# A hybrid decoder layer on one core: single-row states decayed by Scalar and added in one piece, two attention components' scores in one bank, a mask added as a product, and the end of memory attention in another order

## The chip, the cores and the metric

The kernel runs on one core of a Trainium2 chip. The metric is the device time of one execution in microseconds; before the change three runs gave 938.86, 939.27 and 941.57 us, a median of 939.27.

The engines have short names in what follows: PE is TensorE, the matrix engine, with PEld for its weight loads; DVE is VectorE, ACT is ScalarE, POOL is GpSimd, and SP is SyncE, whose queue issues nearly all DMAs. Each engine works through its own list of instructions in order, and waits where the next one's inputs or buffers are not ready.

## The reference, cut to what matters

One layer of a decoder trunk is computed for a prompt (512 tokens) and for 8 samples of 4 new tokens each, with the same weights. The four places that the change touches compute this:

```python
# 1. mLSTM heads (4 x 128): state of each sample and head
C_new = decay[..., None, None] * C + jnp.einsum('bhsd,bhse->bhde', wk, vc)

# 2. differential attention (4 heads, two components c of 64 dims)
s = jnp.einsum('bqhcd,bkhcd->bhcqk', q, k) * (DA_QK_DIM ** -0.5)
s = jnp.where(mask, s, -jnp.inf)
p = jax.nn.softmax(s, axis=-1)
a = p[:, :, 0] - lam * p[:, :, 1]
return jnp.einsum('bhqk,bkhd->bqhd', a, v)

# 3. attention to 256 memory tokens (4 heads x 256), then w_mo
p = jax.nn.softmax(jnp.einsum('bqhd,bkhd->bhqk', q, k) * (MEM_HEAD_DIM ** -0.5), axis=-1)
o = jnp.einsum('bhqk,bkhd->bqhd', p, mv).reshape(B, T, D_MODEL)
return o @ w_mo
```

The prompt's mask is causal (a query sees keys up to its own position). A sample's queries see 256 cached keys and, causally, its 4 new ones. A gated feed-forward part with a depthwise convolution over time follows; its convolution state, weights and bias are small arrays.

## The kernel before

The layer runs in stages on one core, with the matrix engine as the common thread: the mixer's input projection and the mLSTM heads (to 244 us), differential attention (244 to 300), its output projection, memory attention (430 to 475), the w_mo projection (from 476), and the feed-forward part to the end. Products of the projections are made in three terms of two-part numbers: a weight tile in f32 (`wst`, 512 KB by DMA) is cast by ScalarE into a high part and by VectorE, which subtracts that, into a low part, both in a slot `wslot` (four slots, lines 146 and 147). The product lines 411, 412 and 413 use them.

PSUM is split into two pools: five banks tagged "mm" (`mmp`) and three tagged "at" (`at`). A tile of a pool waits until the user of its bank that many tiles ago has been read. Six stage buffers of 4 KB a partition hold `wst` tiles. The order of each engine's list is not the order of the code: a scheduler with a timeline of its own picks it, within the data's dependences, priorities, and `tc.issue_after(x)`, which keeps what is recorded in it behind the instruction x.

The places that the change touches:

- **mLSTM state of the samples** (`mls_update`, lines 1002 to 1011). Eight pieces (two groups of four samples, four heads). Each is one product `mlus` (line 1006) into an "at" bank and four VectorE instructions of 128 columns (line 1008), one for each sample, that multiply its state (held in a `wst` buffer) by its decay and add its part of the product. The state then goes out by DMA and frees its buffer.
- **Differential attention of the prompt** (`da_soft`, lines 1247 to 1265): 16 units, a unit being a block of 128 queries and one head, with 128, 256, 384 or 512 keys. For each of the two components one bank `sda` gets the scores (line 1256) and, by a product of the identity with the mask `cb` in bf16 (line 1257), the mask on the last 128 keys. VectorE takes the row maximum (line 1259), ScalarE the exponentials (line 1260), VectorE joins the components (line 1264); later units of the pipe transpose the result (`tpa`, line 1272, copied to `aT` by line 1274) and multiply by the values (`oda`, line 1284).
- **Differential attention of the samples** (`dk_turn`, `dk_scores`, lines 1220 to 1245): cached keys are transposed (`tpk`, line 1228, copied to `kT` by ScalarE and VectorE in turn, line 1229); the scores `ssc` of two samples each (line 1241) get the mask of the new tokens by a VectorE add of 128x4 (line 1244).
- **Memory attention.** The prompt's part is a pipe of eight units: scores `sca` (line 1454), exponentials `cp` (line 1461), transposes `cpt` (line 1473), values `cpo` (line 1485). Between them stand the samples' scores `ssc` (`mk_scores`, line 1527, from `wst` and `kvt` tiles of the cache), their sum and softmax (`mem_softmax`, with the transposes `spt` and the copies `caz`, line 1576), and their values `pso` (`mv_out`, line 1593): first the values that lie in `wst` buffers, then those in `kvt`. Code lines 1644 to 1659 set how the prompt's pipe and `pso` alternate; `NMID` is 3 and sets how many steps of the pipe come between the softmax and `pso`.
- **Loads around it.** `W.pump()` requests the first four tiles of w_mo. `cr` gets the convolution's state, weights and bias by 24 small DMAs (`conv_in`, lines 1674 to 1676); seven transposes `cvp` (line 1688) read it behind the first matmuls of w_mo. `before` (line 1140) loads five blocks `xb` of the residual for the sum behind w_mo.

Of the kernel before, what the change touches and what calls it, by code (L numbers as in the profile page):

```python
# [7 lines left out]
F32 = mybir.dt.float32  # L8
# [7 lines left out]
P = 128  # L16
# [3 lines left out]
TS = 4  # L20
NS = NB * TS
ROWS = SEQ + NS
H = 4
# [54 lines left out]
def kernel(ctx: ExitStack, tc: tile.TileContext, I, O):  # L78
# [146 lines left out]
    def slotA(w, k0, n0, nrow=256, share=False):  # L225
        def emit():
            st, s = v2(stage(), 512), slot_tile()
            sv = s.rearrange("p l (k n) -> p l k n", k=2)
            r0 = k0 * P
            if nrow == 256:  # L230
                dma(out=st, in_=w[r0:r0 + 256, n0:n0 + 512].rearrange("(k p) n -> p k n", p=P))
                split_w(sv, st, share)
            else:
                dma(out=st[:, 0, :], in_=w[r0:r0 + P, n0:n0 + 512])
                for p0 in (0, 64):
                    dma(out=st[p0:p0 + 64, 1, :], in_=w[r0 + P:r0 + P + 64, n0:n0 + 512])
                split(sv[:, 0], sv[:, 1], st)
            return sv, st
        W.add(emit)
# [113 lines left out]
    class Fill:  # L353
# [8 lines left out]
        def run(self, amount=1e9):  # L362
            while amount > 0 and self.q:
                try:
                    amount -= next(self.q[0])
                except StopIteration:
                    self.q.pop(0)
# [634 lines left out]
    def mls_update(i):  # L1002
        g, h = i // H, i % H
        cs_t = csts[g, h]
        pu = at("mlus")
        mm(pu, lhsT=kS[:, h, :], rhs=vzs[i], start=True, stop=True)
        for b in range(4):
            STT(out=cs_t[:, b, :], in0=cs_t[:, b, :], scalar=dec[:, h, 4 + 4 * g + b:5 + 4 * g + b], in1=pu[:, b * P:(b + 1) * P],
                op0=MUL, op1=ADD)
        dma(out=O["s_ml_C"][0, 4 * g:4 * g + 4, h].rearrange("b d e -> d b e"), in_=cs_t)  # L1010
        F.run(2.5)

    run(pipe(2 * H, mls_values, lambda i: None, lambda i: None, mls_update))
    r, ss = gq[:, 14:15], gq[:, 15:16]
    STT(out=r, in0=den, scalar=-1.0, in1=den, op0=MUL, op1=MAX)
    VTT(out=r, in0=r, in1=gq[:, 2:3], op=MAX)
# [102 lines left out]
    def proj_add(xt, gname, src, gname2, dst, order=None, scale=None):  # L1119
# [20 lines left out]
        def before(b):  # L1140
            for c in [4, 0, 1, 2, 3] if scale else [b]:
                if c not in xb:
                    xb[c] = N("xb")[:rows(c)[1]]
                    dma(out=xb[c], in_=src(c))

        def ev1(b, ps):
            c0, n = rows(b)
# [74 lines left out]
    def dk_turn(b):  # L1222
        kt = kts[b] = wp.tile([P, H, 260], F32, name="kT", tag="W")
        nc.gpsimd.tensor_copy(out=kt[:, :, 256:260], in_=dkT[:, :, SEQ + TS * b:SEQ + TS * (b + 1)])
        for g in range(2):
# [2 lines left out]
                tr(ps[:, h * P:(h + 1) * P], kst[b][g][:, h * P:(h + 1) * P], ident)  # L1228
            (VCP if g else nc.scalar.copy)(out=kt[:, :, g * P:(g + 1) * P], in_=v2(ps, P))

    def dk_scores(b):

        if b % 2 == 0:
            return
        pair = {}
        t = None
        for c in (b, b - 1):
            pair[c] = mmp("ssc")[:, :260]
            for h in range(H):
                with burst(t):  # L1240
                    t = mm(pair[c][NS * h:NS * h + NS], lhsT=qz[:, h, c // 4].rearrange("p c r -> p (c r)"), rhs=kts[c][:, h, :],
                           start=True, stop=True).ins
        for c, ps in pair.items():
            VTT(out=ps[:, 256:260], in0=ps[:, 256:260], in1=con("cm4"), op=ADD)
            sample_exp(sall, c, ps, nm, su)

    def da_soft(i):
        b, h = i // H, i % H
        c0 = b * P
        nk = c0 + P  # L1250
        pt = pts[i] = N("pda").rearrange("p (c k) -> p c k", c=2)
        nm = small(2, "nm")
        su = small(2, "su")
        sv = [mmp("sda")[:, :nk] for _ in range(2)]
        for c in range(2):
            mm(sv[c], lhsT=(dqz if c else dqT)[:, h, c0:c0 + P], rhs=dkT[:, h, 0:nk], start=True, stop=False)
            mm(sv[c][:, c0:nk], lhsT=identb, rhs=cmaskb, start=False, stop=True)
        for c in range(2):
            VRED(out=nm[:, c:c + 1], in_=sv[c], axis=AX.X, op=MAX, negate=True)
            ACT(out=pt[:, c, :nk], in_=sv[c], func=AF.Exp, bias=nm[:, c:c + 1], accum_out=su[:, c:c + 1])  # L1260
        rc = sm.tile([P, 2], F32, name="rc", tag="rc", bufs=6)
        nc.vector.reciprocal(out=rc, in_=su)
        VTS(out=rc[:, 1:2], in0=rc[:, 1:2], scalar1=su[:, 0:1], scalar2=nlam, op0=MUL, op1=MUL)
        STT(out=pt[:, 0, :nk], in0=pt[:, 1, :nk], scalar=rc[:, 1:2], in1=pt[:, 0, :nk], op0=MUL, op1=ADD)
        rcs[i] = rc
# [138 lines left out]
    for t in qx[0] + [both]:  # L1404
        nc.gpsimd.memset(t, 0.0)
    qh, ql = [], []
    selG = cst.tile([P, P], F32, name="selG")
    s32 = T2([P, 32], "selg")
    VRED(out=v2(s32, TS), in_=ident.rearrange("p (n g t) -> p n t g", n=NB, g=4), axis=AX.X, op=ADD)
    VCP(out=selG.rearrange("p (n g t) -> p n g t", n=NB, g=4), in_=v2(s32, TS).unsqueeze(2).broadcast_to([P, NB, 4, TS]))  # L1410
# [98 lines left out]
    def mk_scores(bs):  # L1509

        t = None
        ps = {b: mmp("ssc")[:, :256] for b in bs}
        for e in range(2):
            if e and bs[0] == 0:
                next(prompt)
# [127 lines left out]
    mk_sum(t)  # L1643
    with tc.high_priority():
        mem_softmax()
    for _ in range(NMID):
        next(prompt, None)
    pso = mmp("pso")[:, :256]
    for n0 in (0, 512):
# [1 line left out]
    W.nslots = NSLOT  # L1651
    mv_out(VORD[:6])
    W.pump()
    next(prompt, None)
    next(prompt, None)
    mv_out(VORD[6:])
    run(prompt)
    oS = Z("oS")[:, :256]
    nc.scalar.copy(out=oS, in_=pso)
    ps = at("ost")  # L1660
# [16 lines left out]


    cr = N("cr")
    for g in range(6):  # L1680
        conv_in(cr, 20 * g, 0, 896 * g + (64 if g > 2 else 0), 896)
    conv_in(cr, 0, 896, 2688, 64)
    conv_in(cr, 0, 960, 5440, 64)
    for t0 in (0, 4):
        ps = at("cvp")
        nt = min(4, 7 - t0)
# [372 lines left out]
```

## Time and profile before

| | value |
| --- | --- |
| median of three runs | 939.27 us |
| the profiled execution's own time | 938.97 us |
| span of its profile | 937.2 us |
| mean granted clock of TensorE | 0.994 |
| VectorE, ScalarE, GpSimd busy | 65%, 40%, 24% of the span |
| TensorE waits from 244 to 300 us | 3.1 us in all |
| TensorE waits from 430 to 482 us | 4.2 us in all |
| TensorE waits from 482 us to the end | 0.3 us |

Times in the profile count from the span's start. A wait is the time in which an engine stands still and what released it; "PE mm L411 <- ACT wslot L146" is TensorE at line 411, released by ScalarE's write of wslot in line 146. The granted clock is the share of TensorE's full speed that its throttle let through; a matmul at half the clock takes twice as long and still counts as busy. The time of a row in the timeline includes the pipeline's depth, so that the starts of two matmuls lie closer than one lasts.

### The profile page before, as it was taken

What the parts mean: (1) busy time and instruction counts of PE and PEld (TensorE: products, weight loads), DVE (VectorE), ACT (ScalarE), POOL (GpSimd) and SP (SyncE); (2) the same over time, 40 slices, a digit from 0 to 9 for tenths busy, and PEclk for the clock granted to TensorE, in tenths of its full rate; (3) what the DMA queues carried; (4) which work ended last, traced back from release to release, by engine and by line L of the source; (5) the groups of instructions that cost most, each with busy time, mean ns of one, the idle gap of its engine ahead of it and who ended that gap; (6) DMA issues with size and microseconds to landing.
All of it is one profiled execution on the core that took longest, in us unless ns stands there. A gap on an engine that the chain in (4) does not pass through costs nothing. (4 is left out here: it accounts for less than half of the span.)

```text
span 937.2 us, 17472 instructions
## 1 busy us (share of the span) xinstructions
PE 914.7 (98%) x6780; PEld 798.0 (85%) x6780; DVE 607.5 (65%) x1128; ACT 377.7 (40%) x728; POOL 223.4 (24%) x475
## 2 busy tenths in 40 slices
PE   8999999999999999999999999999999999999995
PEld 5899787879866778998767899889988998999974
DVE  5845144565887438687545778637747785776767
ACT  5745233344586447724434533332212222222232
POOL 6611000024442116581000553001100110110114
PEclk9999999999999999999999999999999999999998
DMA  8950023335780439956766632062054304412023
GB/s 282 320 182 5 1 90 138 91 105 159 246 294 7 137 117 299 321 189 232 283 231 166 202 116 69 26 180 69 22 140 133 89 10 116 133 49 90 24 94 118
DMA packets 120834, 130.59 MB, mean 139 GB/s; under 512 B 8599, under 2 KB 86264, under 8 KB 120752
## 3 DMA queue, kind: packets, MB, share of 16 engines
q1 hardware_dynamic: 114568, 125.96, 42.5%
q10 hardware_dynamic: 6184, 3.53, 1.2%
q8 instruction: 53, 0.87, 0.4%
q14 instruction: 29, 0.24, 0.1%
HBM read 112.54 MB, written 16.93 MB: 138 GB/s over the span
## 5 line engine op out<-in xcount | busy, mean ns | idle before, releaser
L146 ACT CAST wslot<-wst 128x1024 fp32r<-128x1024 f32 x125 | 130.7, 1049 | 265.5 <-issue 72.6
L485 PE MATMUL mm<-fT,wslot 128*128 128x256 f32 x1872 | 235.9, 288 | 0.0
L485 PEld LDWEIGHTS mm<-fT,wslot 128*128 128x128 f32 x1872 | 234.4, 188 | 1.8 <-issue 0.8
L147 DVE TENSOR_TENSOR wslot<-wst,wslot 128x1024 fp32r<-128x1024 f32 x125 | 154.5, 1239 | 85.4 <-ACT wslot L146 84.8
L1865 PE MATMUL mm<-wslot,act 128*128 128x512 f32 (+1 forms) x180 | 69.3, 387 | 0.0
L1868 PE MATMUL mm<-wslot,act 128*128 128x512 f32 (+1 forms) x172 | 67.1, 391 | 0.0
L1869 PE MATMUL mm<-wslot,act 128*128 128x512 f32 (+1 forms) x172 | 66.8, 392 | 0.0
L1767 POOL COPY cvo<-u 128x2 f32<-128x2 f32 x43 | 10.4, 242 | 217.1 <-DVE u L1765 217.1
L411 PE MATMUL mm<-wslot,hT 128*128 128x512 f32 x128 | 51.3, 402 | 0.0
L413 PE MATMUL mm<-wslot,hT 128*128 128x512 f32 x128 | 51.0, 399 | 0.0
L485 PE MATMUL mm<-hT,wslot 128*128 128x256 f32 (+1 forms) x384 | 50.9, 289 | 0.0
L412 PE MATMUL mm<-wslot,hT 128*128 128x512 f32 x128 | 50.8, 397 | 0.0
L1762 DVE TENSOR_TENSOR u<-mm,rsb 128x256 f32<-128x256 f32 x43 | 18.1, 423 | 48.8 <-PE mm L485 48.7
L485 PEld LDWEIGHTS mm<-hT,wslot 128*128 128x128 f32 x384 | 49.2, 188 | 0.5 <-issue 0.2
L1865 PEld LDWEIGHTS mm<-wslot,act 128*128 128x128 f32 x180 | 34.3, 191 | 8.0 <-issue 0.8
L1869 PEld LDWEIGHTS mm<-wslot,act 128*128 128x128 f32 x172 | 32.3, 188 | 6.9 <-issue 0.4
L1868 PEld LDWEIGHTS mm<-wslot,act 128*128 128x128 f32 x172 | 32.3, 188 | 6.9
L1779 ACT ACTIVATE c<-c 128x560 f32<-128x560 f32 x21 | 14.1, 672 | 56.8 <-DVE c L1773 56.7
L1773 DVE SCALAR_TENSOR_TENSOR c<-u,cvT,c 128x560 f32<-128x560 f32 x43 | 34.3, 798 | 0.9
L1772 DVE SCALAR_TENSOR_TENSOR c<-u,cvT,c 128x560 f32<-128x560 f32 x43 | 34.1, 793 | 0.2
L1880 DVE TENSOR_TENSOR yp<-mm,yp 128x512 f32<-128x512 f32 (+1 forms) x41 | 27.1, 673 | 4.8 <-PE mm L1869 4.6
L413 PEld LDWEIGHTS mm<-wslot,hT 128*128 128x128 f32 x128 | 24.1, 188 | 5.0
(497 smaller groups left out, 1859.1 us busy)
## 6 DMA issues: line engine op xcount, KB each, us to landing
wst<-in_w_up_dram SPq DMA_DIRECT2D x42, 512.0 KB
wst<-in_w_in_dram SPq DMA_DIRECT2D x28, 512.0 KB
wst<-in_w_down_dram SPq DMA_DIRECT2D x20, 512.0 KB
kvt<-in_cache_mem_k_dram SPq DMA_DIRECT2D x10, 512.0 KB
kvt<-in_cache_mem_v_dram SPq DMA_DIRECT2D x10, 512.0 KB
wst<-in_w_mk_dram SPq DMA_DIRECT2D x8, 512.0 KB
xb<-in_x_prompt_dram SPq DMA_DIRECT2D x8, 512.0 KB
wst<-in_cache_dk_dram SPq DMA_DIRECT2D x16, 256.0 KB
```

Source lines behind the costliest of these rows:

```text
L146: nc.scalar.copy(out=hi, in_=src)
L147: (eng or nc.vector).tensor_tensor(out=lo, in0=src, in1=f32(hi), op=SUB)
L411: mm(ps[b], lhsT=xt.hi(k, c0, c0 + n), rhs=s[:, 0, kk, :], start=(k == 0), stop=False)
L412: mm(ps[b], lhsT=xt.hi(k, c0, c0 + n), rhs=s[:, 1, kk, :], start=False, stop=False)
L413: return mm(ps[b], lhsT=xt.lo(k, c0, c0 + n), rhs=s[:, 0, kk, :], start=False, stop=(k == nk - 1))
L485: mm(ps[i], lhsT=s[:, l, k, :], rhs=x(k, c0, c1), start=(k == 0 and j == 0), stop=(k == 7 and j == 2))
L1772: STT(out=c, in0=u[:, 1:EXT - 1], scalar=w[1], in1=c, op0=MUL, op1=ADD)
L1773: STT(out=c, in0=u[:, 0:EXT - 2], scalar=w[0], in1=c, op0=MUL, op1=ADD)
L1865: mm(ps, lhsT=t[:, 0, c0:c0 + P], rhs=s[:, 0, i % 2, cs], start=st, stop=False)
L1868: mm(ps, lhsT=t[:, 0, c0:c0 + P], rhs=s[:, 1, i % 2, cs], start=False, stop=False)
L1869: return mm(ps, lhsT=t[:, 1, c0:c0 + P], rhs=s[:, 0, i % 2, cs], start=False, stop=en)
L1880: VTT(out=y, in0=ps, in1=y, op=ADD)
```

## The change

The decay of a sample's state moves from VectorE to ScalarE (32 multiplications in a stage of the pipe ahead of the product), and VectorE adds the product to four states in one instruction of 512 columns. In the units of differential attention with 128 and 256 keys both components' scores share one bank: first a product of the identity with zeros and mask (`cmz`) writes the whole of it, then both components' scores are added, then one instruction takes both maxima. The new tokens' mask is added to the samples' scores by a bf16 product with the identity instead of by VectorE. The samples' scores of memory attention move from the "mm" to the "at" banks. At the end of memory attention one more step of the prompt's pipe runs ahead of `pso`, the rest of it between the two halves of `pso`, and `cr` and `xb` are loaded behind the first w_mo tiles.

```diff
@@ -228,7 +228,7 @@
             sv = s.rearrange("p l (k n) -> p l k n", k=2)
             r0 = k0 * P
             if nrow == 256:
-                dma(out=st, in_=w[r0:r0 + 256, n0:n0 + 512].rearrange("(k p) n -> p k n", p=P))
+                W.last = dma(out=st, in_=w[r0:r0 + 256, n0:n0 + 512].rearrange("(k p) n -> p k n", p=P))
                 split_w(sv, st, share)
             else:
                 dma(out=st[:, 0, :], in_=w[r0:r0 + P, n0:n0 + 512])
@@ -1004,13 +1004,17 @@
         cs_t = csts[g, h]
         pu = at("mlus")
         mm(pu, lhsT=kS[:, h, :], rhs=vzs[i], start=True, stop=True)
-        for b in range(4):
-            STT(out=cs_t[:, b, :], in0=cs_t[:, b, :], scalar=dec[:, h, 4 + 4 * g + b:5 + 4 * g + b], in1=pu[:, b * P:(b + 1) * P],
-                op0=MUL, op1=ADD)
+        VTT(out=cs_t, in0=cs_t, in1=v2(pu, P), op=ADD)
         dma(out=O["s_ml_C"][0, 4 * g:4 * g + 4, h].rearrange("b d e -> d b e"), in_=cs_t)
         F.run(2.5)
 
-    run(pipe(2 * H, mls_values, lambda i: None, lambda i: None, mls_update))
+    def mls_decay(i):
+        g, h = i // H, i % H
+        for b in range(4):
+            c = csts[g, h][:, b, :]
+            nc.scalar.mul(out=c, in_=c, mul=dec[:, h, 4 + 4 * g + b:5 + 4 * g + b])
+
+    run(pipe(2 * H, mls_values, mls_decay, lambda i: None, mls_update))
     r, ss = gq[:, 14:15], gq[:, 15:16]
     STT(out=r, in0=den, scalar=-1.0, in1=den, op0=MUL, op1=MAX)
     VTT(out=r, in0=r, in1=gq[:, 2:3], op=MAX)
@@ -1141,7 +1145,8 @@
             for c in [4, 0, 1, 2, 3] if scale else [b]:
                 if c not in xb:
                     xb[c] = N("xb")[:rows(c)[1]]
-                    dma(out=xb[c], in_=src(c))
+                    with tc.issue_after(loads) if scale else nullcontext():
+                        dma(out=xb[c], in_=src(c))
 
         def ev1(b, ps):
             c0, n = rows(b)
@@ -1228,6 +1233,12 @@
                 tr(ps[:, h * P:(h + 1) * P], kst[b][g][:, h * P:(h + 1) * P], ident)
             (VCP if g else nc.scalar.copy)(out=kt[:, :, g * P:(g + 1) * P], in_=v2(ps, P))
 
+    cm4b = cst.tile([P, TS], BF16, name="cm4b")
+    cmz = cst.tile([P, P], F32, name="cmz", tag="cmz").bitcast(BF16)
+    nc.gpsimd.memset(cmz[:, :P], 0.0)
+    nc.gpsimd.tensor_copy(out=cmz[:, P:], in_=cmaskb)
+    nc.gpsimd.tensor_copy(out=cm4b, in_=con("cm4"))
+
     def dk_scores(b):
 
         if b % 2 == 0:
@@ -1239,9 +1250,11 @@
             for h in range(H):
                 with burst(t):
                     t = mm(pair[c][NS * h:NS * h + NS], lhsT=qz[:, h, c // 4].rearrange("p c r -> p (c r)"), rhs=kts[c][:, h, :],
-                           start=True, stop=True).ins
+                           start=True, stop=False).ins
         for c, ps in pair.items():
-            VTT(out=ps[:, 256:260], in0=ps[:, 256:260], in1=con("cm4"), op=ADD)
+            with burst(t):
+                t = mm(ps[:, 256:260], lhsT=identb, rhs=cm4b, start=False, stop=True).ins
+        for c, ps in pair.items():
             sample_exp(sall, c, ps, nm, su)
 
     def da_soft(i):
@@ -1251,12 +1264,21 @@
         pt = pts[i] = N("pda").rearrange("p (c k) -> p c k", c=2)
         nm = small(2, "nm")
         su = small(2, "su")
-        sv = [mmp("sda")[:, :nk] for _ in range(2)]
+        if b < 2:
+            both = v2(mmp("sda")[:, :2 * nk], nk)
+            sv = [both[:, 0], both[:, 1]]
+            mm(both, lhsT=identb, rhs=cmz[:, 2 * P - nk:].unsqueeze(1).broadcast_to([P, 2, nk]), start=True, stop=False)
+        else:
+            sv = [mmp("sda")[:, :nk] for _ in range(2)]
         for c in range(2):
-            mm(sv[c], lhsT=(dqz if c else dqT)[:, h, c0:c0 + P], rhs=dkT[:, h, 0:nk], start=True, stop=False)
-            mm(sv[c][:, c0:nk], lhsT=identb, rhs=cmaskb, start=False, stop=True)
+            mm(sv[c], lhsT=(dqz if c else dqT)[:, h, c0:c0 + P], rhs=dkT[:, h, 0:nk], start=b > 1, stop=b < 2 and c == 1)
+            if b > 1:
+                mm(sv[c][:, c0:nk], lhsT=identb, rhs=cmaskb, start=False, stop=True)
+        if b < 2:
+            VRED(out=nm, in_=both, axis=AX.X, op=MAX, negate=True)
         for c in range(2):
-            VRED(out=nm[:, c:c + 1], in_=sv[c], axis=AX.X, op=MAX, negate=True)
+            if b > 1:
+                VRED(out=nm[:, c:c + 1], in_=sv[c], axis=AX.X, op=MAX, negate=True)
             ACT(out=pt[:, c, :nk], in_=sv[c], func=AF.Exp, bias=nm[:, c:c + 1], accum_out=su[:, c:c + 1])
         rc = sm.tile([P, 2], F32, name="rc", tag="rc", bufs=6)
         nc.vector.reciprocal(out=rc, in_=su)
@@ -1404,7 +1426,7 @@
     for t in qx[0] + [both]:
         nc.gpsimd.memset(t, 0.0)
     qh, ql = [], []
-    selG = cst.tile([P, P], F32, name="selG")
+    selG = cst.tile([P, P], F32, name="selG", tag="cmz")
     s32 = T2([P, 32], "selg")
     VRED(out=v2(s32, TS), in_=ident.rearrange("p (n g t) -> p n t g", n=NB, g=4), axis=AX.X, op=ADD)
     VCP(out=selG.rearrange("p (n g t) -> p n g t", n=NB, g=4), in_=v2(s32, TS).unsqueeze(2).broadcast_to([P, NB, 4, TS]))
@@ -1509,7 +1531,7 @@
     def mk_scores(bs):
 
         t = None
-        ps = {b: mmp("ssc")[:, :256] for b in bs}
+        ps = {b: at("ssc")[:, :256] for b in bs}
         for e in range(2):
             if e and bs[0] == 0:
                 next(prompt)
@@ -1643,7 +1665,7 @@
     mk_sum(t)
     with tc.high_priority():
         mem_softmax()
-    for _ in range(NMID):
+    for _ in range(NMID + 1):
         next(prompt, None)
     pso = mmp("pso")[:, :256]
     for n0 in (0, 512):
@@ -1651,10 +1673,9 @@
     W.nslots = NSLOT
     mv_out(VORD[:6])
     W.pump()
-    next(prompt, None)
-    next(prompt, None)
+    loads = W.last.ins
+    run(prompt)
     mv_out(VORD[6:])
-    run(prompt)
     oS = Z("oS")[:, :256]
     nc.scalar.copy(out=oS, in_=pso)
     ps = at("ost")
@@ -1677,10 +1698,11 @@
 
 
     cr = N("cr")
-    for g in range(6):
-        conv_in(cr, 20 * g, 0, 896 * g + (64 if g > 2 else 0), 896)
-    conv_in(cr, 0, 896, 2688, 64)
-    conv_in(cr, 0, 960, 5440, 64)
+    with tc.issue_after(loads):
+        for g in range(6):
+            conv_in(cr, 20 * g, 0, 896 * g + (64 if g > 2 else 0), 896)
+        conv_in(cr, 0, 896, 2688, 64)
+        conv_in(cr, 0, 960, 5440, 64)
     for t0 in (0, 4):
         ps = at("cvp")
         nt = min(4, 7 - t0)
```

`W.last` is the load that `W.pump()` requested last, so `loads` is the fourth load of w_mo.

**TensorE at the end of memory attention.** These are its rows from the transposes of the samples' softmax (`spt`) into the gemm of w_mo (lines 411 to 413), before:

```order
L1573 MATMUL spt<-cpk,spc 32x32 x32
L1593 MATMUL pso<-wst,caz 32x256 x24
L1473 MATMUL cpt<-cpk,cp 128x128 x4
L1593 MATMUL pso<-kvt,caz 32x256 x40
L1485 MATMUL cpo<-pT,mvN 128x512 x12
L411 MATMUL mm<-wslot,oT_5340 128x512 x2
L412 MATMUL mm<-wslot,oT_5340 128x512
```

and after the change:

```order
L1595 MATMUL spt<-cpk,spc 32x32 x32
L1495 MATMUL cpt<-cpk,cp 128x128 x4
L1615 MATMUL pso<-wst,caz 32x256 x24
L1507 MATMUL cpo<-pT,mvN 128x512 x12
L1615 MATMUL pso<-kvt,caz 32x256 x40
L411 MATMUL mm<-wslot,oT_5329 128x512 x4
L412 MATMUL mm<-wslot,oT_5329 128x512
```

The group of transposes `cpt` moved from behind the first part of `pso` to ahead of it, and the values `cpo` from behind `pso` into its middle; the same work stands in front of w_mo.

**SyncE's queue around the w_mo loads.** Before, from the last small loads to the feed-forward weights (`w_up`):

```order
L1675 DMA cr<-in_w_dw_dram 3x64
L1676 DMA cr<-in_b_dw_dram 1x64
L1144 DMA xb<-x_d_2551 32x1024
L1144 DMA xb<-x_d_2551 128x1024
L231 DMA wst<-in_w_mo_dram 128x2x512 x6
L1144 DMA xb<-x_d_2551 128x1024 x3
L231 DMA wst<-in_w_mo_dram 128x2x512 x2
L254 DMA wst<-in_w_up_dram 128x8x128 x8
```

After, from the cache's values for memory attention to the first of the small loads:

```order
L1605 DMA wst<-in_cache_mem_v_dram 128x1024 x6
L1605 DMA kvt<-in_cache_mem_v_dram 128x1024 x10
L231 DMA wst<-in_w_mo_dram 128x2x512 x4
L1695 DMA cr<-in_state_conv_dram 16x896
L1696 DMA cr<-in_w_dw_dram 3x896
L1697 DMA cr<-in_b_dw_dram 1x896
```

Before, the 24 small loads began between the eighth and ninth `kvt` load, and two `xb` loads followed them ahead of w_mo. Now four w_mo loads stand directly behind the ten `kvt` loads, then come the 24 small ones, two more of w_mo, the five `xb` and the last two of w_mo.

**TensorE where differential attention begins.** Its rows behind the last two state products (`mlus`): scores and masks of the prompt's first two units, transposes of cached keys (`tpk`) and the turn of the mLSTM output (`mlt`). Before:

```order
L1006 MATMUL mlus<-vz,kS 128x512 x2
L1256 MATMUL sda<-dkT,dqT 128x128
L1257 LDWEIGHTS cb
L1257 MATMUL sda<-cb 128x128
L1256 MATMUL sda<-dkT,dqz 128x128
L1257 LDWEIGHTS cb
L1257 MATMUL sda<-cb 128x128
L1256 MATMUL sda<-dkT,dqT 128x128
L1228 MATMUL tpk<-cpk,wst 128x128 x4
```

and after the change:

```order
L1006 MATMUL mlus<-vz,kS 128x512 x2
L1270 LDWEIGHTS cb
L1270 MATMUL sda<-cmz,cb 128x256
L1274 MATMUL sda<-dkT,dqT 128x128
L1274 MATMUL sda<-dkT,dqz 128x128
L1233 MATMUL tpk<-cpk,wst 128x128 x4
L1270 LDWEIGHTS cb
L1270 MATMUL sda<-cmz,cb 128x256
L1274 MATMUL sda<-dkT,dqT 128x128
```

A unit's two mask products of 128 columns became one of 256 ahead of the scores, and the first keys' transposes moved from inside the second unit to between the two.

## The prediction

> **What bounds the kernel.** I read the page first. TensorE is the limit: the line below gives its busy time and share.
>
> ```profile
> span 937.2 us, 17472 instructions
> PE 914.7 (98%) x6780; PEld 798.0 (85%) x6780; DVE 607.5 (65%) x1128; ACT 377.7 (40%) x728; POOL 223.4 (24%) x475
> ```
>
> That leaves 937.2 − 914.7 = 22.5 us in which TensorE has nothing, at the start, at the end and in short gaps. No edit removes much matrix work, so the change can win only gaps, and slow clock hidden inside "busy" time. So next I read TensorE's waits in the two stages that the diff touches: differential attention (244 to 300 us), then memory attention and the start of w_mo (430 to 482 us). Columns: who waited for whom, total us, times, longest.
>
> ```profile
> PE tpa L1272 <- DVE pda L1264: 1.4, 2, 1.1
> PE oda L1284 <- ACT aT L1274: 0.9, 1, 0.9
> PE tpk L1228 <- ACT kT L1229: 0.5, 1, 0.5
> PE tpk L1228 <- DVE kT L1229: 0.3, 1, 0.3
> ...
> PE mm L411 <- ACT wslot L146: 1.4, 1, 1.4
> PE sca L1454 <- ACT cp L1461: 1.1, 1, 1.1
> PE pso L1593 <- ACT caz L1576: 0.6, 1, 0.6
> PE ssc L1527 <- DVE ql L1438: 0.6, 1, 0.6
> PE mm L412 <- DVE wslot L147: 0.5, 1, 0.5
> ```
>
> The first four, 3.1 us, are the first stage; the other five, 4.2 us, the second. From 482 us to the end TensorE waits once:
>
> ```profile
> PE mm L472 <- ACT fT L146: 0.3, 1, 0.3
> ```
>
> Last, the end of memory attention in TensorE's timeline (start, length, work, wait before it), with two matmuls of the same gemm at a later time, and four microseconds of its start (TensorE, weight loads, DVE, ACT and POOL busy, granted clock, DMA share, GB/s).
>
> ```profile
> 464.14 2.80 PE L1593 MATMUL pso<-wst,caz 128*32 128x256 f32 x48 [0.62 <-ACT caz L1576]
> 466.87 0.66 PE L1473 MATMUL cpt<-cpk,cp 128*128 128x128 f32 x4
> 467.45 4.52 PE L1593 MATMUL pso<-kvt,caz 128*32 128x256 f32 x80
> 471.91 3.05 PE L1485 MATMUL cpo<-pT,mvN 128*128 128x512 f32 x12
> 476.33 0.73 PE L411 MATMUL mm<-wslot,oT 128*128 128x512 f32 x2 [1.38 <-ACT wslot L146]
> ...
> 481.50 0.47 PE L411 MATMUL mm<-wslot,oT 128*128 128x512 f32 x1
> ...
> 482.02 0.89 PE L1688 MATMUL cvp<-cpk,cr 120*128 120x120 f32 x7
> ...
> 511.99 0.39 PE L411 MATMUL mm<-wslot,oT 128*128 128x512 f32 x1
> 512.22 0.40 PE L412 MATMUL mm<-wslot,oT 128*128 128x512 f32 x1
> ...
> 478.00:482.00 4.00, 4.00 (x13) 3.12 (x12) 3.70 (x4) 3.22 (x5) 0.00 (x0) 0.57 1.05 405
> ```
>
> The reader is to see two losses. The gemm starts late, because its first weight slot is not cast. Then it runs at a granted clock of 0.57, which the page counts as busy: 4 × 0.43 = 1.7 us more that no wait shows.
>
> **The change part by part, from the end backwards.**
>
> *Loads and order at the end of memory attention.* SyncE's queue and ScalarE show why the slot is late:
>
> ```profile
> 450.76 0.33 SPq L1674 DMA_DIRECT2D cr<-in_state_conv_dram  x1
> 451.99 0.26 SPq L1675 DMA_DIRECT2D cr<-in_w_dw_dram  x1
> ...
> 468.13 0.78 SPq L1144 DMA_DIRECT2D xb<-x_d  x2
> 469.00 4.96 SPq L231 DMA_DIRECT2D wst<-in_w_mo_dram  x6
> ...
> 475.24 1.04 ACT L146 CAST wslot<-wst 128x1024 fp32r<-128x1024 f32 x1 [6.44 <-DMA wst<-in_w_mo_dram]
> ...
> 476.31 3.88 DVE L147 TENSOR_TENSOR wslot<-wst,wslot 128x1024 fp32r<-128x1024 f32 x3 [7.06 <-ACT wslot L146]
> ...
> 464.00:469.00 5.00, 4.86 (x82) 2.83 (x86) 1.23 (x4) 0.83 (x3) 0.00 (x0) 1.00 0.14 32
> ```
>
> The first w_mo load is issued at 469.00, behind 24 small cr loads and two xb loads, and lands at 475.24, 6.2 us later, with the xb bytes ahead of it. After the change it stands directly behind the last kvt load, and its stage buffer comes free when the first values of pso<-wst have been read, some half a microsecond into that group: I put its issue at 464.6. Landing takes at most the 6.2 us of that row (470.8); without the xb bytes (640 KB, some 1.6 us at 405 GB/s) and with DMA engines that are nearly free from 464 to 469 (last row) I expect some 3.5 to 4.5 (468 to 469). A cast of 1.04 and a DVE remainder of 1.3 (3.88 / 3) make the slot ready at 470 to 473. TensorE gets there at 474.95 (471.91 + 3.05) less the gain of the next paragraph, 474.4. So the wait goes even by the slow bound. The later slots follow 1.3 us apart (512 KB at the 405 GB/s of the window of 478 to 482), and the six matmuls that use up a slot take 1.4. In its place the twelve matmuls between 474.95 and 481.50 take 12 × 0.23 = 2.8 us (pitch: 512.22 − 511.99) instead of 6.55: **−3.75**, of which 1.38 + 0.53 are waits and 1.7 the clock.
>
> [...]
>
> *One cpt group ahead of pso<-wst.* TensorE waits 0.62 there for the caz copy. The cpt group now stands in that gap; it held TensorE from 466.87 to 467.45, 0.58. Its casts on ScalarE come after the caz copies, so they delay nothing: **−0.6**, and nothing if cp were late, which it was not (cpt ran without a wait).
>
> *Sample scores in the other pool of banks.* The ssc tiles leave the five "mm" banks. So the second ssc need not wait for ql's evictions (0.62) nor the following sca for a bank that exps hold (1.07): **−1.7**. What is late next are the "at" banks, three of them: the fourth ssc needs the copy of the first out of its bank, which ScalarE now makes two rows earlier. If that copy came as late as before, the wait would come back whole; bounds 0 and −1.7, and I take −1.7, since TensorE's order here is unchanged and the first ssc ends well before the fourth starts.
>
> *Decay on ScalarE.* Rows: busy us, mean ns, idle before.
>
> ```profile
> L1008 DVE SCALAR_TENSOR_TENSOR wst<-wst,dec,mlus 128x128 f32<-128x128 f32 x32 | 8.9, 344 | 2.7 <-PE mlus L1006 2.4
> L1045 DVE TENSOR_TENSOR mltm<-mlt,soT 128x512 f32<-128x512 f32 x4 | 2.6, 678 | 0.0
> ...
> L1286 ACT ACTIVATE dao<-oda,rc 128x128 f32<-128x128 f32 x12 | 4.6, 380 | 0.7 <-PE oda L1284 0.7
> ...
> 244.09 2.16 DVE L1008 SCALAR_TENSOR_TENSOR wst<-wst,dec,mlus 128x128 f32<-128x128 f32 x8 [1.53 <-PE mlus L1006]
> ...
> 230.00:243.70 13.70, 13.70 (x122) 13.25 (x111) 11.02 (x33) 1.83 (x5) 9.99 (x13) 1.00 0.46 135
> ```
>
> 32 instructions of 0.344 become eight adds of 0.68: 11.0 to 5.4 us of durations. ScalarE gets 32 multiplies of at most 0.38, 12 us; the window shows it busy 1.83 of the 13.7 us before 243.7, so nearly all of them lie beside the mixer's gemm, which holds TensorE whole. Only the last two of the eight pieces count: their eight instructions ended at 246.25, where the first score maxima queue behind them; two adds, 1.36, save 0.8 us of DVE there. The adds now wait for ScalarE too, and behind the multiplies on ScalarE stand the square for numS and two copies of soT, which free "mm" banks of the gemm. If one state's four multiplies (1.5 us) were late, the next mlus would lack its bank and TensorE would stand still for up to as long; I cost that at nothing, since ScalarE is through with its 12 us at about the gemm's end even so, and with most states well before.
>
> *Two components in one bank, masks by products.*
>
> ```profile
> L1257 PE MATMUL sda<-cb 128*128 128x128 bf16 x32 | 7.0, 219 | 0.0
> L1244 DVE TENSOR_TENSOR ssc<-ssc,cpk 128x4 f32<-128x4 f32 x8 | 1.2, 162 | 0.0
> L1259 DVE TENSOR_REDUCE nm<-sda 128x1 f32<-128x256 f32 x8 | 3.3, 417 | 0.5 <-PE sda L1257 0.4
> L1259 DVE TENSOR_REDUCE nm<-sda 128x1 f32<-128x512 f32 x8 | 5.4, 686 | 0.7 <-PE sda L1257 0.6
> ...
> 250.00:260.00 10.00, 9.67 (x93) 7.43 (x94) 9.96 (x30) 8.22 (x30) 6.20 (x9) 1.00 1.01 350
> ```
>
> Eight units change. With 128 keys, two mask products of 128 columns become one of 256, the same columns. With 256 keys they become one of 512: twice the columns. A 128-column product is at most 0.22, so TensorE gets at most 4 × 0.44 = 1.8 more; as matmuls overlap, I count columns instead: a quarter of the 0.23 that 512 columns of w_mo take is 0.06 for 128, by which the four units cost 4 × 0.12 = 0.5. The eight products for the new tokens cost at most 8 × 0.22 = 1.8; I take 0.06 each for the least step of the array, 0.5, though they have only four columns. So TensorE gets +1.0 (0 to 3.6). DVE loses eight adds, 1.3 us, and in a unit of 256 keys two reductions of 0.417 become one of 0.686, for which the first exp of the unit now waits. That helps where DVE is full, 9.96 of 10 us from 250 to 260. It feeds two of the four waits above (pda 1.4, kT 0.3, together 1.7); the ScalarE waits (1.4) stay. I take 1.4 of the 1.7 as won, all of it but the 0.3 for kT, since the change takes DVE work from in front of it: **−0.4** for the stage, between −3.1 (all four waits won, the products free) and +3.6.
>
> **The sum.** −3.75 − 0.6 − 1.7 − 0.4 = −6.4 us. The profiled execution took 938.97 (span 937.2 and 1.8 around it), 0.3 below the median of three, 939.27. So 938.97 − 6.4 = **932.6**. The rest passes through because TensorE is never idle behind 482 but for 0.3 us, and what feeds it is released by its own gemms.
>
> **Rivals.** *The clock drop stays.* [...] Against: it begins just behind the only gaps above 1.1 us of the stage, and ends when matmuls have run closely. Then 1.7 is not won: 934.3.
>
> *The early load buys nothing.* If w_mo's landing were bound by HBM traffic rather than its place in the queue, the 3.75 stay: 936.3. Against: the DMA engines are busy for 0.14 of 464 to 469, where w_mo now goes.
>
> *Given back later.* The one wait behind 482, for fT (0.3), stands at the end of a chain of norms, stores and weight casts at 522 to 546 us. It has no slack, so an order in it that doesn't follow TensorE takes the gain. If two thirds of the 6.4 go there: 936.8.
>
> *cr late, slower than before.* The 18 cr loads that cvp transposes now wait behind w_mo's first four. Issued from 467 on at the 0.33 us that one takes there, they are all out by 473 and land before cvp, which stands at 481 once twelve matmuls are through. But with large loads in flight the trace has them 1.23 us apart (450.76 to 451.99). At that pace, from 467 on, 18 take 22 us: 489, and TensorE waits 8 us behind cvp, then loses the 1.7 of a clock drop: 932.6 + 9.7 = 942.3. It decides at a pace above (481 − 2 − 467) / 18 = 0.67 us. Against: four large loads are in flight there, not ten.
>
> **Numbers.** Forecast 0.63; clock stays 0.09; load buys nothing 0.09; given back 0.12; cr late 0.07. Faster and slower are counted from 0.3%, 2.8 us, about what a measurement of this kernel can tell from no change: 936.4 and 942.1. The first two and some of the third are faster, 0.78; the rest of the third and the fourth the same, 0.15; the last slower, 0.07. The range reaches up past "given back" and down to an attention stage that wins most of its bound of 3.1: 930.0 to 937.5.
>
> **What would show it.** Right: no wait of L411 for wslot, clock 1.00 at the gemm's start, no wait of ssc and sca for ql and cp, pso<-wst right behind cpt, each about 6 us earlier by then. Wrong: a wait of cvp for cr; sca or ssc waiting for sc copies; waits of tpa or oda longer by over 1 us; the fT wait behind 540 grown by microseconds.

## The result, and the profile after

The changed kernel takes 936.47 us (median of 8 runs, 935.33 to 937.54), the kernel before 940.67 us in the same runs (938.86 to 942.77): a ratio of 0.9956, 95% interval 0.9944 to 0.9968, or about 4.2 us less. Forecast were 6.4 us less, to 932.6, with a range to 937.5. The direction was right and the gain a third smaller.

The profiled execution of the changed kernel took 937.25 us, so 1.8 lie around its span of 935.5. One profile of each kernel (937.2 and 935.5) shows only 1.7 us of difference, since executions of one kernel differ by up to 4 us; so what follows compares lengths of stages within a profile, over several profiles.

The page's first lines, after:

```profile
span 935.5 us, 17462 instructions
PE 913.4 (98%) x6780; PEld 797.5 (85%) x6780; DVE 602.2 (64%) x1088; ACT 386.9 (41%) x760; POOL 223.8 (24%) x478
```

VectorE lost 5 us of work and ScalarE gained 9: the state update moved as meant. TensorE is as full as before. Its waits after, in the attention stage (first five), in the gemm that makes the queries q ahead of memory attention (`ql` is their low part, which VectorE writes), and in memory attention and the start of w_mo (waiting line, what it waited for, total us, times, longest):

```profile
PE tpk L1233 <- ACT kT L1234: 1.5, 1, 1.5
PE tpa L1294 <- DVE pda L1286: 1.0, 1, 1.0
PE oda L1306 <- ACT aT L1296: 0.9, 1, 0.9
PE sda L1270 <- ACT pda L1282: 0.6, 1, 0.6
PE ssc L1252 <- DVE rc L1285: 0.2, 1, 0.2
...
PE mm L485 <- DVE ql L1460: 1.4, 1, 1.4
...
PE ssc L1549 <- issue: 0.6, 1, 0.6
PE sca L1476 <- issue: 0.4, 1, 0.4
```

The five old waits of memory attention and w_mo are gone. In their place stand two that end on "issue", which means that the profile shows nothing that TensorE waited for. The attention stage has more waits than before (4.2 us for 3.1). The end of memory attention in TensorE's timeline, with SyncE's queue and ScalarE beside it:

```profile
465.48 0.76 PE L1595 MATMUL spt<-cpk,spc 128*32 128x32 f32 x64
466.17 0.66 PE L1495 MATMUL cpt<-cpk,cp 128*128 128x128 f32 x4
466.86 2.80 PE L1615 MATMUL pso<-wst,caz 128*32 128x256 f32 x48
...
477.04 1.21 PE L411 MATMUL mm<-wslot,oT 128*128 128x512 f32 x4
...
479.94 0.40 PE L411 MATMUL mm<-wslot,oT 128*128 128x512 f32 x1
...
483.43 0.88 PE L1710 MATMUL cvp<-cpk,cr 120*128 120x120 f32 x7
...
467.56 1.92 SPq L231 DMA_DIRECT2D wst<-in_w_mo_dram  x4
...
474.65 0.32 SPq L1695 DMA_DIRECT2D cr<-in_state_conv_dram  x1
476.65 0.24 SPq L1696 DMA_DIRECT2D cr<-in_w_dw_dram  x1
...
480.03 0.25 SPq L1697 DMA_DIRECT2D cr<-in_b_dw_dram  x1
...
474.59 3.90 ACT L146 CAST wslot<-wst 128x1024 fp32r<-128x1024 f32 x4 [1.31 <-PE pso L1615]
...
478.00:482.00 4.00, 4.00 (x19) 3.25 (x18) 2.30 (x3) 0.75 (x2) 0.00 (x0) 1.00 0.23 57
```

w_mo starts without a wait and at a granted clock of 1.00 (it was 0.57). The casts are held by `pso`, not by the DMA: the slots share their buffers with the `kvt` tiles that `pso` reads. The small cr loads crawl, up to 2.0 us apart, while the w_mo loads drain; the 18th is issued at 480.03, 3.4 us ahead of the transposes that need it. What SyncE's queue waited for among them, by line (total us, times, longest):

```profile
SPq L1696 <- DMA wst<-in_w_mo_dram: 2.1, 2, 1.7
SPq L1695 <- DMA wst<-in_w_mo_dram: 1.5, 1, 1.5
SPq L1697 <- DMA wst<-in_w_mo_dram: 1.0, 1, 1.0
```

### The profile page after: what moved, and what is told of

The parts are those of the page before. It is cut to its first block, busy times and chain, and to the rows that moved or that the text cites. A ratio compares the mean times of both kernels' runs of the same rounds, so it can differ in the third digit from the quotient of the medians.

```text
span 935.5 us, 17462 instructions
## 1 busy us (share of the span) xinstructions
PE 913.4 (98%) x6780; PEld 797.5 (85%) x6780; DVE 602.2 (64%) x1088; ACT 386.9 (41%) x760; POOL 223.8 (24%) x478
## 5 line engine op out<-in xcount | busy, mean ns | idle before, releaser
L411 PE MATMUL mm<-wslot,hT 128*128 128x512 f32 x128 | 51.3, 402 | 0.0
L412 PE MATMUL mm<-wslot,hT 128*128 128x512 f32 x128 | 50.8, 397 | 0.0
```

Source lines behind the costliest of these rows:

```text
L411: mm(ps[b], lhsT=xt.hi(k, c0, c0 + n), rhs=s[:, 0, kk, :], start=(k == 0), stop=False)
L412: mm(ps[b], lhsT=xt.hi(k, c0, c0 + n), rhs=s[:, 1, kk, :], start=False, stop=False)
```

## The experiments

Three lengths, each between two starts on TensorE, tell the parts apart better than the whole time: the attention stage (first `sda` to the first matmul of w_out, the output projection behind it), the sample scores and what follows them (first `ssc` to first `spt`), and the end (first `spt` to the 13th matmul of w_mo).

| kernel | attention | ssc to spt | end |
| --- | --- | --- | --- |
| before, two profiles | 55.37, 55.37 | 30.56, 30.40 | 18.75, 18.50 |
| changed, two profiles | 56.24, 56.22 | 30.13, 29.63 | 14.46, 14.46 |
| no mixer edits | 55.37 | 29.86 | 14.46 |
| scores in the old banks | 56.23 | 30.27 | 14.47 |
| old end | 56.22 | 29.92 | 15.78 |
| banks alone | 55.37 | 29.95 | 15.96 |
| new end alone | 55.36 | 30.45 | 14.42 |
| no decay on ScalarE | 56.04 | 29.44 | 14.46 |
| 16 more warm-up matmuls | 56.23 | 30.10 | 14.47 |
| no shared bank | 56.60 | 29.50 | 14.46 |
| no mask product for new tokens | 56.01 | 28.84 | 14.46 |
| old order of the loads | 56.22 | 29.06 | 15.88 |

**The changed kernel again.** No edit.

> The changed kernel once more, for a second profile of it. Its first profile shows three stalls that the prediction didn't have: 1.39 us of the q gemm waiting for VectorE's ql, and 0.63 and 0.4 us of the sample scores and the prompt's scores waiting for 'issue'. Theory A (chance of one execution: the cache loads landed late, instructions were fetched late): the 1.39 us wait is not there again or has another size by over 0.5 us, and the time is about 4.2 us below the kernel before. Theory B (they belong to the new order): all three come back with the same size within 0.2 us.

Measured: 935.42 us against 939.37 (ratio 0.996, 0.9945 to 0.9975). The waits are there again: 1.3 for ql, 0.7 for "issue". Theory A's change of size didn't come for those two; the stop of `sca` did not come back, so theory B isn't met either. The ql wait is still no property of the order: kernels whose orders are the same up to there have it at 0.2 (scores in the old banks) and at none (old end), and one without the mixer edits (new end alone) has it at 1.0. Ahead of it VectorE's transposes wait for cache loads, in the first profile:

```profile
416.94 1.25 DVE L1529 STREAM_TRANSPOSE wst<-wst 128x1024 f32<-128x1024 f32 x1 [1.91 <-DMA wst<-in_cache_mem_k_dram]
```

A single profile holds or lacks over 1 us by it. That instructions were fetched late, as theory A has it beside the loads, no trace shows.

**The mixer edits undone.**

```diff
-        VTT(out=cs_t, in0=cs_t, in1=v2(pu, P), op=ADD)
+        for b in range(4):
+            STT(out=cs_t[:, b, :], in0=cs_t[:, b, :], scalar=dec[...], in1=pu[...], op0=MUL, op1=ADD)
...
-        if b < 2:
-            both = v2(mmp("sda")[:, :2 * nk], nk)
+        sv = [mmp("sda")[:, :nk] for _ in range(2)]
...
-                t = mm(ps[:, 256:260], lhsT=identb, rhs=cm4b, start=False, stop=True).ins
+            VTT(out=ps[:, 256:260], in0=ps[:, 256:260], in1=con("cm4"), op=ADD)
```

> The changed kernel with the three edits of the mixer undone (state update by VectorE alone, one bank for each component, new tokens' mask by VectorE); banks and end as changed. The prediction gave these edits -0.4 us: then this kernel is 0.4 us slower than the changed one. Theory B from the first profile (TensorE reaches the output projection 1.26 us later than before): these edits cost 1.3 us, so this kernel is 1.3 us faster than the changed one and about 5.5 us below the kernel before.

Measured: 934.42 us (0.9951, 0.9936 to 0.9966), 1.0 less than the changed kernel on the same chip, and the attention stage is back at 55.37. So the mixer's edits cost 0.86 us in their own stage instead of winning 0.4. It has the lowest median of the kernels timed more than once, but its interval overlaps the changed kernel's.

**The sample scores back in the old banks.**

```diff
-        ps = {b: at("ssc")[:, :256] for b in bs}
+        ps = {b: mmp("ssc")[:, :256] for b in bs}
```

> The changed kernel with the sample scores of memory attention back in the mm banks; TensorE, VectorE and SyncE have the same order as in the changed kernel. The prediction: the waits for ql (0.62) and for the exponentials' bank (1.07) come back, 1.7 us slower than the changed kernel. Rival: the stall only moves on to the at banks or to later waits, and the time is within 0.5 us of the changed kernel.

Measured: 936.33 us (0.9971, 0.9958 to 0.9983), 0.9 more than the changed kernel. The old waits return (sca for the exponentials 1.1, ssc for ql 0.4) and both "issue" waits are gone. That is neither number of the expectation but about half of the 1.7; the two intervals overlap, so the 0.9 is uncertain.

**The old end.** The order of the loads goes back to the old one (its edit is in the last experiment), and so do the steps of the pipe:

```diff
-    for _ in range(NMID + 1):
+    for _ in range(NMID):
...
-    loads = W.last.ins
-    run(prompt)
+    next(prompt, None)
+    next(prompt, None)
     mv_out(VORD[6:])
+    run(prompt)
```

> The changed kernel with the end of memory attention as before (the steps of the prompt's pipe and the order of the cr, xb and w_mo loads); mixer and banks as changed. The prediction gave this part -3.75 - 0.6 = -4.35 us: this kernel is 4.35 us slower than the changed one, with the first w_mo matmul waiting over 1 us and the clock near a half behind it. Rival (an early load buys nothing): within 1 us of the changed kernel.

Measured: 937.97 us (0.999, 0.9978 to 1.0001), 2.55 more than the changed kernel. Neither expectation: L411 doesn't wait and the clock stays at 1.00. The rows say why (TensorE's timeline; the clock of 478 to 482):

```profile
472.98 3.04 PE L1506 MATMUL cpo<-pT,mvN 128*128 128x512 f32 x12
475.91 0.74 PE L411 MATMUL mm<-wslot,oT 128*128 128x512 f32 x2
477.17 0.51 PE L412 MATMUL mm<-wslot,oT 128*128 128x512 f32 x1 [0.52 <-DVE wslot L147]
...
478.00:482.00 4.00, 3.79 (x21) 2.80 (x20) 3.76 (x5) 3.01 (x6) 0.00 (x0) 1.00 1.03 386
```

TensorE comes about 1 us later than in the kernel before (475.91 against 474.95), just as the slot gets ready. So the late tile costs 18.75 − 14.46 = 4.3 us where TensorE is early, and 15.78 − 14.46 = 1.3 where it is late by that microsecond.

**The kernel before again.** No edit.

> The kernel before, for a second profile of it. The prediction counted 1.7 us of the end's 3.75 as a clock drop that follows from the late w_mo tile. In the kernel with the old end and the new rest the drop was absent (clock 1.00 from 476 on), though w_mo was late there too. Theory A (the drop follows from the gaps in the kernel before): the granted clock is again below 0.7 in 478 to 482. [...]

Measured: 938.26 us (0.9995, 0.9979 to 1.0011). The gap and the clock are there again:

```profile
476.25 0.77 PE L411 MATMUL mm<-wslot,oT 128*128 128x512 f32 x2 [1.28 <-ACT wslot L146]
477.51 0.51 PE L412 MATMUL mm<-wslot,oT 128*128 128x512 f32 x1 [0.49 <-DVE wslot L147]
...
478.00:482.00 4.00, 4.00 (x14) 3.02 (x13) 3.74 (x5) 3.15 (x5) 0.00 (x0) 0.57 1.05 406
```

In both profiles of this kernel the drop follows the two gaps, 1.3 to 1.4 and 0.5 us, and in no profile without the first of them is it there. The clock is at a half for 3.4 us in each (the first profile, then this one):

```profile
478.24:481.65 3.41, 3.41 (x10) 2.67 (x9) 3.11 (x4) 2.98 (x5) 0.00 (x0) 0.50 1.05 402
...
478.33:481.75 3.42, 3.42 (x10) 2.54 (x9) 3.16 (x4) 2.83 (x5) 0.00 (x0) 0.50 1.05 405
```

In these 3.4 us the matmuls of w_mo start 0.43 us apart (478.94 to 481.50 in the first profile, 478.72 to 481.28 in this one, six steps in 2.56 us each), and 0.23 apart at 1.00 (482.98 to 485.30 in the first profile, ten steps in 2.32). That is 1.8 times as far, not twice; by it the drop costs 1.6 us, by the share of the clock 1.7. TensorE counts as busy all the while.

The drop behind the gaps is what theory A says. That these gaps bring it in every execution is not shown. Every timed execution has its mean granted clock on record, and 3.4 us at a half take 0.002 off it. These two profiles have 0.994; the twelve others have 0.995 to 0.997, but for the one with 16 more warm-up matmuls (0.994, and 1.00 from 478 to 492 us). Of the ten executions of this run eight have 0.996 or 0.997. Of all 75 executions of the kernel before with a clock on record, 19 have 0.994 or less, with a median of 940.06 us, and 44 have 0.996 or more, with 938.22. If the lower clock is this drop, it comes by estimate in a quarter to two fifths of the executions (19 of 75, or 31 with the 12 at 0.995), and these are 1.8 us longer. Whether the others lack the gaps too, or have them without the drop, no trace shows.

**Banks alone, and the new end alone.** The kernel before with the one-line edit of the banks; and with the edits of the end.

> The kernel before with one edit alone: the sample scores in the at banks. Theory A (parts add up): about 0.9 us below the kernel before, as taking this edit out of the changed kernel cost 0.9. Theory B (the w_mo tile lands at a time that SyncE's queue sets, not TensorE): TensorE reaches w_mo up to 1.2 us earlier and waits that much longer there, so L411's wait grows from 1.4 to over 2 us and the time is within 0.4 us of the kernel before.

> The kernel before with the new end alone (steps of the pipe, order of the loads). The prediction's own step gave 4.35 us. Theory A (parts add up): 4.95 - 0.9 = 4.0 us below the kernel before. Theory B (clock drop not always there, and the cpt step buys less): 2.5 to 3.3 us below.

Measured: banks alone 936.8 us against 938.7 (0.9976, 0.9961 to 0.999), new end alone 935.48 (0.9961, 0.9944 to 0.9979). Both theories on the banks miss, A's 0.9 by little (the interval begins at 0.9). The edit won 0.5 us between `ssc` and `spt`, but this execution reached the scores 1.2 us later than the first one of the kernel before, 0.5 of it a wait for ql. So TensorE came to w_mo just late enough: no wait of L411, no clock drop (end 15.96 for 18.6). The new end alone won 3.2 us in the runs, near the upper end of theory B's range, with an interval that holds theory A too. Alone they won 1.9 and 3.2; together, in the kernel without the mixer edits, 4.6 by the ratio, so their times add up within the noise. In the new end's profile the end is 4.2 us shorter, of which a ql wait of 1.0 is given back ahead of it.

**No decay on ScalarE, no shared bank, no mask product.** Each undoes one mixer edit of the changed kernel alone.

> The changed kernel with the state update by VectorE alone. One look, read by the length of the attention stage on TensorE, from the first score to the first w_out matmul, which is 55.37 us before and 56.22 to 56.24 in four kernels with all the mixer's edits. Theory A (ScalarE's 32 multiplies are hidden, the other two edits cost): still 56.2 with a wait of 1.5 us of tpk for ScalarE's kT copy. Theory B (the decay makes it): 55.4 or less, without that wait.

> The changed kernel with one bank for each component again; decay by ScalarE and the new tokens' product stay. Read by the attention stage, first score to first w_out matmul: 55.37 us before, 56.23 with all three edits, 56.04 without the decay. ScalarE still has four exponentials ahead of the second and third kT copies. Theory A (this order costs, and it comes with the decay): the tpk wait of 1.5 us for ScalarE's kT stays, stage 55.9 to 56.5. Theory B (the shared bank costs): stage within 0.2 of 55.37.

> The changed kernel with the new tokens' mask by VectorE again; decay by ScalarE and shared bank stay. Theory A (the eight products with their weight loads are free, as TensorE's busy time in the stage did not grow): stage within 0.2 of 56.23. The prediction's price of 0.06 each: 55.7.

Measured (one execution each: 934.41, 936.17 and 936.51 us): stages of 56.04, 56.60 and 56.01. The decay does set the wait for kT, by an order: with it ScalarE has four exponentials ahead of two copies, without it a copy after every two. ScalarE's timeline of the changed kernel (the sums behind the first two exponentials left out), the two copies in the kernel without the decay, then TensorE's wait in the one and in the other:

```profile
247.61 0.37 ACT L1282 ACTIVATE pda<-sda,nm 128x128 f32<-128x128 f32 x1
...
247.97 0.36 ACT L1282 ACTIVATE pda<-sda,nm 128x128 f32<-128x128 f32 x1
...
248.31 0.36 ACT L1282 ACTIVATE pda<-sda,nm 128x128 f32<-128x128 f32 x1
248.56 0.21 ACT L1282 ACTIVATION_READ_ACCUMULATOR pda<-sda,nm 128x1 f32 x1
248.66 0.37 ACT L1282 ACTIVATE pda<-sda,nm 128x128 f32<-128x128 f32 x1
248.91 0.21 ACT L1282 ACTIVATION_READ_ACCUMULATOR pda<-sda,nm 128x1 f32 x1
249.00 1.08 ACT L1234 COPY kT<-tpk 128x512 f32<-128x512 f32 x2
```

```profile
248.35 0.58 ACT L1230 COPY kT<-tpk 128x512 f32<-128x512 f32 x1
...
249.51 0.61 ACT L1230 COPY kT<-tpk 128x512 f32<-128x512 f32 x1
```

```profile
249.65 0.66 PE L1233 MATMUL tpk<-cpk,wst 128*128 128x128 f32 x4 [1.54 <-ACT kT L1234]
```

```profile
248.99 0.66 PE L1229 MATMUL tpk<-cpk,wst 128*128 128x128 f32 x4 [0.68 <-ACT kT L1230]
```

Yet only 0.2 of the 0.86 goes with the decay: the wait shrinks by 0.9, and TensorE is busy for 0.8 more. The shared bank wins 0.4 beside the other two (without it the wait for kT stays and the stage is 56.60, 0.1 above theory A's bound), and the mask product costs 0.2, just outside what theory A there allowed. No single edit makes the 0.86; that one of them does was wrong, and how they act together is open.

**16 more warm-up matmuls.**

```diff
-    NWARM, NFILL = 9, 7
+    NWARM, NFILL = 25, 7
```

> The changed kernel with 16 more idle matmuls of the warm-up at its start, so that every later instruction of TensorE stands 16 matmuls (with their weight loads) further on in its stream. With the sample scores in the at banks, TensorE stops for 0.63 to 0.79 us behind the 77th or 78th matmul of one group of them, released by nothing that the profile shows, in six profiles; without, in none of four. [...] Theory B (a wait on data or a bank): it stays behind the 77th or 78th.

The whole time (944.66, one execution) carries the added work at the start. The stop, in TensorE's timelines of the changed kernel, this one, the one without the shared bank (eight products more ahead) and the one without the new tokens' products (eight less), each followed by the group behind it:

```profile
438.40 1.32 PE L1549 MATMUL ssc<-wst,qx 128*32 128x64 f32 x78
440.35 0.47 PE L1549 MATMUL ssc<-wst,qx 128*32 128x64 f32 x17 [0.63 <-issue]
```

```profile
444.12 1.09 PE L1549 MATMUL ssc<-wst,qx 128*32 128x64 f32 x63
446.06 0.69 PE L1549 MATMUL ssc<-wst,qx 128*32 128x64 f32 x33 [0.85 <-issue]
```

```profile
438.04 1.20 PE L1537 MATMUL ssc<-wst,qx 128*32 128x64 f32 x69
440.06 0.58 PE L1537 MATMUL ssc<-wst,qx 128*32 128x64 f32 x26 [0.82 <-issue]
```

```profile
438.84 1.43 PE L1545 MATMUL ssc<-wst,qx 128*32 128x64 f32 x86
440.49 0.35 PE L1545 MATMUL ssc<-wst,qx 128*32 128x64 f32 x9 [0.22 <-issue]
```

78, then 63, 69 and 86: 16 matmuls more ahead move the stop up by 15, eight more by 9, eight less down by 8. It stands at a fixed place in the stream, not at a tile or a bank. Counted from the start, it comes behind 3,124 to 3,126 matmuls in all ten profiles that have it (0.22 to 0.85 us long); a second, shorter stop (0.20 to 0.43 us) comes exactly 256 matmuls later in the five that have that too, four times at `sca` and once at `ssc` (behind 3,125 and 3,381 in the changed kernel's first profile). So theory B is refuted; what TensorE lacks there the profile doesn't show. In the four profiles where TensorE stands still for the ql and bank waits (1.5 to 1.7 us in all) in the same stretch, the stop is absent; that these waits cover it is inferred from that.

**The old order of the loads.** Steps of the pipe as changed, `issue_after(loads)` taken out.

```diff
-                    with tc.issue_after(loads) if scale else nullcontext():
-                        dma(out=xb[c], in_=src(c))
+                    dma(out=xb[c], in_=src(c))
...
-    with tc.issue_after(loads):
-        for g in range(6):
+    for g in range(6):
```

> The changed kernel with the old order of the cr, xb and w_mo loads; the pipe's steps, banks and mixer stay. The prediction: the first w_mo tile is late again. Theory A (SyncE's queue sets its landing): its cast starts at about 475 again, at most 0.5 us before TensorE gets there in this kernel, with a wait of L412 of 0.5 and up to 2 us lost in all; 1 to 2.5 us slower than the changed kernel. Rival (the steps of the pipe do it): within 0.5 us of the changed kernel.

Measured: 937.28 us (0.9977, 0.9962 to 0.9991), 1.6 to 2.0 more than the changed kernel by the ratios (0.9977 against 0.9960 and 0.9956 of 939). The tile is late again, ScalarE and TensorE:

```profile
477.16 1.04 ACT L146 CAST wslot<-wst 128x1024 fp32r<-128x1024 f32 x1 [3.77 <-DMA wst<-in_w_mo_dram]
...
478.25 1.20 PE L411 MATMUL mm<-wslot,oT 128*128 128x512 f32 x4 [1.03 <-ACT wslot L146]
```

A gap of 1.03 here left the clock at 1.00; the end is 1.4 longer. The order of the loads does it, as theory A has it, though the cast came at 477 and not 475, and the wait is of L411 for the cast, not of L412: the queue's time floats with the cache loads ahead.

## Why the prediction was right, and where its sizes were off

- **The end (−3.75 and −0.6, together −4.35): right.** 18.75 to 14.46 is −4.3 against the first profile of the kernel before, −4.0 against the second. Both waits and the clock drop are gone. Of the two terms only the sum was measured. The cpt group fills the caz gap: spt to pso is 1.4 before and after, and the group no longer stands between the halves of pso. The slot's time was worked out from the wrong thing, which did no harm: I had it ready at 470 to 473 by the landing of its load, but its cast waited for `pso` until 474.59, and the matmul came at 477.04 without a wait. The early load that buys nothing is refuted, and the clock drop did not stay. But the 1.7 that the sum put down to the clock is there only in the executions that have the drop, by the estimate above a quarter to two fifths; and the late tile costs 1.3 instead of 4.3 where TensorE comes a microsecond later.
- **Banks (−1.7): the mechanism right, the size off.** The term measured −0.8: between `ssc` and `spt` ten profiles with the edit average 29.64 us, four without 30.42 (the changed kernel's own two are 0.6 below the two of the kernel before). What the prediction put as "late next", a copy out of the "at" banks, never came. The two waits went whole, but 0.2 to 1.2 us came back as the stops at fixed places of the stream, which the sum put at nothing: less its stops the stretch takes 28.6 to 29.2 us in the ten, less its two waits 28.8 to 28.9 in the four.
- **Mixer (−0.4): the step that failed.** The sum put "TensorE gets +1.0" against "1.4 of the 1.7 as won". The products were nearly free (busy 51.9 us in the stage, 52.2 before), and the waits did not shrink but moved: tpa for pda 1.36 to 1.05, tpk for kT 0.84 to 1.54, and a new one of sda for a bank of ScalarE's exponentials, 0.64. I counted VectorE's load and left ScalarE's order out, though "the ScalarE waits (1.4) stay" rested on it. The 0.06 for each product of four columns, "the least step of the array", was my estimate and no run shows it: without all eight products, and with VectorE's adds back, the stage is 0.2 shorter (56.01 for 56.23). +0.86.
- **The sum.** The three stretches give −4.2 − 0.6 + 0.86 = −3.9 between the two profiles of each kernel, and the runs −4.2 and −4.0. That is in part luck, for the profiles as wholes differ by 2.0 only (936.9 before, 934.9 after, on average). The stretch that the table leaves out, from the first matmul of w_out to the first `ssc`, took 132.7 and 132.8 us before and 134.6 in both profiles of the changed kernel, 1.3 to 1.4 of it the ql wait. The other kernels took 132.7 to 135.0 there, one of them (old end) 133.0 with the changed kernel's order up to that wait; so no edit is shown to cost this, but it is not shown to be chance either. Behind the end nothing was given back: from the 13th matmul of w_mo to the end of the span it is 455.7 and 455.4 us before, 455.5 and 455.3 after, which refutes "given back later".
- **cr late, the slower rival.** It did not happen, but the margin was thinner than I wrote. I had the 18 loads out by 473; the 18th went at 480.03, as the large loads in flight put them up to 2.0 us apart. From the first (469.58) on that is a mean pace of 0.61 us, where the prediction had the loss begin at 0.67.
- **The chances.** The 0.09 for a clock drop that stays was my estimate: no run shows what brings the drop. The measured change, −0.44%, is in "faster" as a ratio. By the bound of 936.4 us, which was worked out from 939.27, the 936.47 would just miss it: the kernel before took 940.67 beside it. That 936.47 lies in the range, 1.0 below its upper end, is owed to the end and to the range's width: the banks bought half of their term, and the mixer had the wrong sign.

## What to carry to other kernels

What a transfer that lands late costs depends on when the engine gets there: here 4.3 us in one profile and 1.3 in another, where the engine came a microsecond later. So price such an edit with and without the others. When load moves from one engine to another, look at the order in which the scheduler then puts the second engine's instructions: a copy that two exponentials overtook made TensorE wait 0.9 us longer. Compare stages, start to start, over several profiles, and add up all of them: here the attention stage repeats to 0.02 us where the whole time moves by 4, but a stretch between two stages differs by up to 2 from profile to profile. And a profile is one execution: look at the mean clock of the others before a clock drop in it goes into a sum.

## What the runs showed of the hardware

TensorE stops for 0.2 to 0.9 us at a fixed place of its instruction stream, behind 3,124 to 3,126 matmuls, in a run of short ones (78 in 1.3 us), in ten profiles; in the four where it stood for 1.5 to 1.7 us in the same stretch it doesn't. And the granted clock fell to 0.5 for 3.4 us, in which the matmuls of w_mo started 0.43 us apart instead of 0.23, behind two gaps of 1.3 to 1.4 and 0.5 us within 2.6 us, in the two profiles of the kernel before. It stayed at 1.00 behind a gap of 1.03 (old order of the loads), one of 0.52 (old end), and the 0.62 and 1.07 at 433 to 436 us of the kernel before. Why there, and why by estimate not in every execution, is open.
